# Four projections instead of two beside the token operands, and another buffer ring for the early norms' scratch

## The chip, the cores and the metric

The kernel runs on one core of one Trainium2 chip. The metric is the device time of one execution in microseconds (us), a median over runs. The core's engines each work through a queue of their own, strictly in the order in which the program was written out: TensorE (PE in the profile) multiplies matrices into PSUM, VectorE (DVE), ScalarE (ACT) and GpSimd (POOL) do the elementwise work, and SyncE (SP) mostly issues transfers. TensorE's clock has two levels here, 1.2 and 2.4 GHz; the column PEclk gives the granted clock as a share of the full one.

## The reference, cut to what matters

One step of one decoder layer: RMS norms, one combined input projection, three parallel branches (sparse attention, a pooling mixer, attention to memory), a merge and a gated feed-forward. The change touches only the beginning, the input projection and the norms of single heads:

```python
def project_inputs(x, l, w):
    z = rmsnorm(x, w['attn_norm_g'][l]) @ w['w_in'][l]
    q, kc, vc, ks, vs, kw, vw, nsa_g, pool_u, mem_q, merge_g = jnp.split(z, _split_points(), axis=-1)
    ...
    q = rmsnorm(q.reshape(b, t, KV_HEADS, GROUP, HEAD_DIM), w['nsa_q_g'][l])
    ks = rmsnorm(kv(ks), w['nsa_ks_g'][l])
    kw = rmsnorm(kv(kw), w['nsa_kw_g'][l])
```

1024 prompt tokens and 8 sample tokens go through the same weights, so the kernel handles T = 1032 tokens of width 1024.

## The kernel before, in words

Every factor of a matrix product is held as a sum of a high and a low part (hi + lo), so each product of a 128x128 weight tile with a chunk of tokens takes three matmuls (hi·hi, hi·lo, lo·hi). Tokens lie along the free dimension, in three chunks of 344; the width of 1024 lies in eight tiles k of 128 partitions.

**Stage 1, the token operands (L331 to L359).** For each chunk and each k: a transfer brings `xr`; ScalarE makes `xh` (L338, x times the norm's gain, high part); VectorE makes `xl` (L339, the rest); the squares of `xr` come from ScalarE or GpSimd (L345, L347) and are summed into `ssq` one after the other, by VectorE and GpSimd in turn (L348). Beside it TensorE runs two projections on each chunk as its operands appear (L354, the keys `ks` and `kw`; weights W01). After a chunk, a matmul with ones (L356) gives the sum of squares over partitions in `ps_p`, and the helper `rsqrt` (L273 to L278) makes `rstd`: VectorE scales (L273), ScalarE takes logarithm, exponential and square (L274 to L276), VectorE corrects by one Newton step (L277, L278). L359 then multiplies the projections by `rstd` into `z`.

**After stage 1.** `proj` loads and splits a weight (L239 ScalarE, L240 VectorE) and runs the four query projections q0 to q3 (L257, 72 matmuls each, into the PSUM ring `ps_t`, L364 multiplies by `rstd`). Each of the six tensors ks, kw, q0 to q3 is then normed head by head by `hnorm`, chunk by chunk, so 18 norms: ScalarE squares (L371), splits the square (L239 into `mg`, low part by GpSimd at L240), TensorE sums over a head's partitions by two matmuls (L380, into `ps_s`), `rsqrt` follows (L273 to L278, result `hn_r`), and VectorE applies it (L383). Then come nine V tiles (L257 with `wvh`, `wvl`: 24 matmuls of 280 columns each, into the same ring `ps_t` of three banks); VectorE empties each into `vtok` (L437) and `gate` (L438), and only then does its bank come free for the third tile after it. L474 sums squares of the memory tokens.

**What sets the order.** The Python code is not the order of the engines: the tile framework simulates the program with its own estimates while it builds, and writes each engine's queue out in the order in which that simulation issued the instructions. So a change in one place can reorder queues elsewhere. Buffers are rings: `T` (12 tiles of T columns: `xr`, `ssq`, `z`, V weights), `H` (4 tiles of 512: `rq_w`, `rq_a`, `hn_r`, `vtok`), `U` (10 tiles of 512: squares), `X` (6 of 512), `mg` (5); PSUM has banks in the tags g (1), s (3), t (3) and p (1).

Of the kernel before, what the change touches and what calls it, by code (L numbers as in the profile page):

```python
# [16 lines left out]
KD = D // 128  # L17
# [3 lines left out]
CH = ((0, 344), (344, 344), (688, 344))  # L21
CW = max(n for _, n in CH)
# [8 lines left out]
NT, NH, NU, NX = 12, 4, 10, 6  # L31
# [162 lines left out]
def body(nc, tc, xT, memT, w_p, w_m, w_v, w_mk, w_mv, w_up, w_un, w_out, w_gu, w_dn, w_pool, w_cmp, gains, consts, jlt,  # L194
         pg_k, pg_v, win_k, win_v, cm_k, cm_v, st_p, pt, ptv, o_y, o_k, o_v, o_wk, o_wv, o_pu, o_ps, o_mk, o_mv):
    from contextlib import ExitStack, nullcontext
    V, S, G, PE, SY = nc.vector, nc.scalar, nc.gpsimd, nc.tensor, nc.sync
    f = lambda a: a.bitcast(F32)
# [13 lines left out]
    def XG(name):  # L212
        return xgp.tile([128, T], F32R, name=name, tag="xg", bufs=16)
# [18 lines left out]
    def gv(n, i=0):  # L232
        return gn[:, _GW[n][0] + i:_GW[n][0] + i + 1]

    def psum(tag="s", dt=F32, w=512):
        return pp.tile([128, w], dt, name="ps_" + tag, tag=tag, bufs=dict(zip(('g', 's', 't', 'p'), PSB))[tag])

    def split(src, hi, lo, he=None, le=None):
        (he or S.copy)(hi, src)  # L239
        (le or V.tensor_sub)(lo, src, f(hi))  # L240

    def wload(src, n, eng=None, le=None, parts=1):
        wr = wp.tile([128, n], F32, name="wr", tag="wr", padded_shape=[128, T])
# [38 lines left out]
    ca = A.enter_context(tc.tile_pool(name="cstA", bufs=1))  # L282
    CWID = consts.shape[1]
    ct = ca.tile([128, CWID], F32, name="ct")
    G.dma_start(ct, consts)

    def C(n):
        o, w, r = _CW[n]
# [3 lines left out]
    st_ = {}  # L292
# [3 lines left out]
    def TT(dt=F32, name="t"):  # L296
        return st_["tp"].tile([128, T], dt, name=name, tag="T", bufs=NT)
# [9 lines left out]
    def TU(name):  # L307
        return st_["tp"].tile([128, 512], F32, name=name, tag="U", bufs=NU)

    def TX(name):  # L310
        return st_["tp"].tile([128, 512], F32R, name=name, tag="X", bufs=NX)
# [2 lines left out]
                                               engine=mybir.EngineType.Activation, ins=[], outs=[]))  # L314


    xh, xl, xr = [], [], []
    ssq = TT(name="ssq")
    rstd = cp.tile([128, T], F32, name="rstd")
    W01 = []  # L320
    ks, kw = TT(name="z"), TT(name="z")

    def xload(k, c):
        (SY, S)[k % 2].dma_start(xr[k][:, c], xT[k][:, c])

    for k in range(KD):
        xr.append(TT(name="xr"))
        xh.append(XG("xh"))
        xl.append(XG("xl"))
    for ci, (c0, n) in enumerate(CH):  # L330
        c = slice(c0, c0 + n)  # L331
        pss = [psum("st"[ci % 2])[:, :n] for _ in range(2)]
        for k in range(KD):
            xload(k, c)
            if ci == 0 and k < 2:
                W01.append(wload(w_p[k], 1024, parts=2))
            h, l = xh[k][:, c], xl[k][:, c]
            S.activation(h, xr[k][:, c], AF.Copy, scale=gv("attn", k))  # L338
            V.scalar_tensor_tensor(l, xr[k][:, c], gv("attn", k), f(h), op0=ALU.mult, op1=ALU.subtract)  # L339
            if k == 0:  # L340
                S.activation(ssq[:, c], xr[k][:, c], AF.Square)
            else:
                sq = TU("sq")[:, :n]
                if k in XG_SQ:
                    G.tensor_mul(sq, xr[k][:, c], xr[k][:, c])  # L345
                else:
                    S.activation(sq, xr[k][:, c], AF.Square)  # L347
                (G if k in XG_ADD else V).tensor_add(ssq[:, c], ssq[:, c], sq)  # L348
        for k in range(KD):
            for t in range(2):  # L350
                wh, wl = W01[t]
                w = slice(k * 128, k * 128 + 128)
                for x, (a, b) in enumerate(((wh, xh), (wh, xl), (wl, xh))):
                    PE.matmul(pss[t], lhsT=a[:, w], rhs=b[k][:, c], start=k == 0 and x == 0, stop=k == KD - 1 and x == 2)  # L354
        ps = psum("p")[:, :n]
        PE.matmul(ps, lhsT=ones, rhs=ssq[:, c], start=True, stop=True)  # L356
        rsqrt(tmp, rstd[:, c], ps, n, 1.0 / D)
        for t, z in enumerate((ks, kw)):
            V.tensor_mul(z[:, c], pss[t], rstd[:, c])  # L359

    def proj(i, src=None, tag="t"):
        wh, wl = wload((w_p if src is None else src)[i], 1024)
        z = TT(name="z")
        gemm(wh, wl, xh, xl, KD, lambda ci, c0, n, ps: V.tensor_mul(z[:, c0:c0 + n], ps, rstd[:, c0:c0 + n]),  # L364
             tag)
        return z

    def hnorm(z, blk, inv, g, cols=CH, split_sq=False):
        for c0, n in cols:
            sq = TU("sq")[:, :n]  # L370
            S.activation(sq, z[:, c0:c0 + n], AF.Square)  # L371
            ps = psum("s")[:, :n]
            if not split_sq:
                PE.matmul(ps, lhsT=blk, rhs=sq, start=True, stop=True)
            else:
                hl = mg(n, F32R), mg(n, F32R)
                split(sq, *hl, le=G.tensor_sub)
                bl = blkr if blk is blk64 else onesr
                for x in range(2):
                    PE.matmul(ps, lhsT=bl, rhs=hl[x], start=x == 0, stop=x == 1)  # L380
            r = tmp([128, 512], name="hn_r")[:, :n]
            rsqrt(tmp, r, ps, n, inv)
            V.scalar_tensor_tensor(z[:, c0:c0 + n], z[:, c0:c0 + n], g, r, op0=ALU.mult, op1=ALU.mult)  # L383

    blk64 = C("blk64")
# [5 lines left out]
    ps = psum("g")  # L391
# [1109 lines left out]
```

## Time and profile before

| | |
|---|---|
| median of 3 runs | 1869.57 us (1867.78 to 1874.47) |
| profiled execution, its own time | 1869.54 us |
| its span (first to last instruction) | 1867.8 us |
| TensorE busy | 1798.3 us, 96% of the span |
| VectorE, ScalarE, GpSimd busy | 65%, 47%, 39% |
| TensorE busy in the first 50 us | 33.5 us |
| last matmul of stage 1 (L354) | 48.27 us |
| first matmul of V tile 4 | 116.08 us |

The profile is of one execution; its time lies 1.7 us over its span and within 0.1 us of the median. Times in the trace count from the first instruction. TensorE is the engine that is nearly always busy; the first 50 us are the one stretch of the early program in which it is idle for a third of the time.

### The profile page before, as it was taken

How to read it: one execution, taken by the hardware profiler on the slowest of the kernel's cores; microseconds unless marked ns; L12 is line 12 of the kernel's file. 1: busy time of each engine (PE TensorE's matmuls, PEld its weight loads, DVE VectorE, ACT ScalarE, POOL GpSimd, SP SyncE). 2: the span in 40 equal slices, each digit the busy share in tenths (PEclk: the TensorE clock that was granted, in tenths of full speed). 3: DMA queues.
4: the chain of work that ended last, by engine and by line, in shares of the span. 5: the costliest groups of instructions: out<-in, count | busy, mean ns of one | idle time of the engine just before them, and what ended most of it. 6: DMA issues, size and time to landing. Idle time of an engine off the chain costs nothing.

```text
span 1867.8 us, 34509 instructions
## 1 busy us (share of the span) xinstructions
PE 1798.3 (96%) x12337; PEld 1729.2 (93%) x12337; DVE 1210.0 (65%) x2748; ACT 870.7 (47%) x2012; POOL 737.5 (39%) x865
## 2 busy tenths in 40 slices
PE   6999999999999999989999999999999999999999
PEld 5998998888988999979989998899999999999999
DVE  8875788663564766778886834866666666636332
ACT  5643766445454676657774545422322223314100
POOL 5300211556341645457753437655545545100000
PEclk9999999899999999989999999999999999999999
DMA  4243124999665111552325643122222222546122
GB/s 162 100 148 139 65 101 164 296 316 315 205 201 169 53 43 63 179 165 78 108 64 177 213 134 100 62 87 78 71 80 80 84 87 69 170 131 184 59 69 94
DMA packets 142366, 241.13 MB, mean 129 GB/s; under 512 B 21449, under 2 KB 100450, under 8 KB 142194
## 3 DMA queue, kind: packets, MB, share of 16 engines
q1 hardware_dynamic: 118722, 189.69, 31.2%
q0 software_dynamic: 8496, 30.23, 4.8%
q10 hardware_dynamic: 14976, 19.01, 2.9%
q8 instruction: 97, 1.59, 0.4%
q14 instruction: 75, 0.61, 0.1%
HBM read 176.31 MB, written 62.55 MB: 128 GB/s over the span
## 4 chain that ended last, share of the span: by engine, by line
PE 55%; DMA 5%; DVE 4%; issue 2%; ACT 2%; POOL 1%; SPq 0%; ACTq 0%; DVEq 0%; POOLq 0%
PE ps_t L257 10%; PE ps_s L1385 10%; PE ps_t L1385 9%; PE ps_g L257 7%; PE ps_s L257 7%; PE ps_p L1061 3%; PE ps_s L1032 3%; PE ps_t L1077 2%; PE ps_g L1385 2%; PE ps_p L1385 2%; DMA mg<-acd 1%; DMA mg<-gd 1%; DMA gt<-gd 1%; DMA olr<-od 1%; DVE t L240 0%
## 5 line engine op out<-in xcount | busy, mean ns | idle before, releaser
L257 PE MATMUL ps_g<-xh,wh 128*128 128x344 f32 x624 | 206.1, 330 | 3.9 <-ACT mg L543 2.3
L257 PE MATMUL ps_g<-xl,wh 128*128 128x344 f32 x624 | 201.7, 323 | 0.0
L257 PE MATMUL ps_g<-xh,wl 128*128 128x344 f32 x624 | 201.6, 323 | 0.0
L239 ACT CAST wh<-wr 128x512 fp32r<-128x512 f32 (+3 forms) x138 | 99.9, 746 | 199.9 <-PE ps_t L257 83.5
L1051 POOL TENSOR_SCALAR P<-P,st,gate 128x384 f32<-128x384 f32 (+2 forms) x192 | 125.6, 664 | 94.6 <-DVE st L1046 37.8
L240 DVE TENSOR_TENSOR wl<-wr,wh 128x512 fp32r<-128x512 f32 (+3 forms) x112 | 105.0, 946 | 56.9 <-ACT wh L239 55.5
L239 ACT CAST cw<-tS 128x512 fp32r<-128x512 f32 x88 | 54.3, 619 | 182.0 <-PE ps_t L1385 98.2
L522 ACT ACTIVATE P<-P,st 128x384 f32<-128x384 f32 (+2 forms) x192 | 112.1, 586 | 40.1 <-DVE st L519 36.3
L257 PEld LDWEIGHTS ps_g<-xh,wh 128*128 128x128 f32 x624 | 118.2, 189 | 9.2 <-ACT mg L543 4.1
L257 PEld LDWEIGHTS ps_g<-xl,wh 128*128 128x128 f32 x624 | 118.5, 190 | 1.1 <-issue 0.4
L257 PEld LDWEIGHTS ps_g<-xh,wl 128*128 128x128 f32 x624 | 118.2, 189 | 1.3 <-issue 0.2
L240 DVE TENSOR_TENSOR ptl<-ps_t,pth 128x512 fp32r<-128x512 f32 (+1 forms) x208 | 108.0, 530 | 15.6 <-ACT pth L239 13.4
L239 ACT CAST pth<-ps_t 128x512 fp32r<-128x512 f32 (+1 forms) x208 | 91.3, 457 | 46.6 <-PE ps_t L1077 29.2
L240 DVE TENSOR_TENSOR cw<-tS,cw 128x512 fp32r<-128x512 f32 x88 | 93.3, 1061 | 29.7 <-ACT cw L239 26.1
L1385 PE MATMUL ps_s<-t,cw 128*128 128x258 f32 x792 | 106.1, 283 | 3.1 <-ACT rq L274 3.1
L1385 PE MATMUL ps_t<-t,cw 128*128 128x258 f32 x792 | 106.8, 283 | 2.1 <-DVE t L240 2.1
L1385 PE MATMUL ps_s<-b,cw 128*128 128x258 f32 x792 | 107.8, 286 | 0.0
L1385 PE MATMUL ps_t<-b,cw 128*128 128x258 f32 x792 | 105.6, 282 | 0.3 <-issue 0.3
L1385 PEld LDWEIGHTS ps_s<-t,cw 128*128 128x128 f32 x792 | 100.0, 190 | 3.3 <-ACT rq L274 3.3
L1385 PEld LDWEIGHTS ps_t<-t,cw 128*128 128x128 f32 x792 | 99.6, 189 | 2.9 <-DVE t L240 2.9
L1385 PEld LDWEIGHTS ps_s<-b,cw 128*128 128x128 f32 x792 | 101.4, 192 | 0.3
L519 DVE CUSTOM_DVE_ANT_0 P<-ps_s,ct 128x384 f32<-128x384 f32 (+3 forms) x160 | 83.2, 530 | 27.0 <-PE ps_t L1077 18.1
(527 smaller groups left out, 5659.0 us busy)
## 6 DMA issues: line engine op xcount, KB each, us to landing
kpg<-pg_k SPq DMA_DIRECT2D x128, 192.0 KB, 4.1
wr<-w_gu SPq DMA_DIRECT2D x44, 512.0 KB, 3.8
gd<-mg ACTq DMA_DIRECT2D x72, 172.0 KB, 3.4
wr<-w_m POOLq DMA_DIRECT2D x24, 512.0 KB, 5.4
acd<-zu SPq DMA_DIRECT2D x44, 258.0 KB, 2.0
mg<-acd SPq DMA_DIRECT2D x66, 172.0 KB, 3.0
mg<-gd SPq DMA_DIRECT2D x48, 172.0 KB, 2.4
wr<-w_p SPq DMA_DIRECT2D x16, 512.0 KB, 3.4
```

The costliest lines, as they stand in the source:

```text
L239: (he or S.copy)(hi, src)
L240: (le or V.tensor_sub)(lo, src, f(hi))
L257: PE.matmul(ps, lhsT=x, rhs=y, start=i == 0, stop=i == n - 1)
L519: V.tensor_tensor_reduce(P[u], s, m, -scale, ini, ALU.add, ALU.min, st[:, u:u + 1])
L522: S.activation(P[u], P[u], AF.Exp, bias=nm, scale=-1.0, accum_out=st[:, 6 + u:7 + u])
L1032: PE.matmul(ps, lhsT=u["q"][:, i * 128:i * 128 + 128], rhs=kk[:, k0 * 128 + a:k0 * 128 + a + n], start=x == 0, stop=x == 1)
L1051: lastp[:] = [G.tensor_scalar(p_, p_, st4[:, j, 5:6], gate[:, q, c:c + 1], op0=ALU.mult, op1=ALU.mult)]
L1061: PE.matmul(pv[:, c0:c0 + n], lhsT=lh, rhs=rhs, start=pvs["n"] == 0, stop=last, skip_group_check=True)
L1077: PE.transpose(pt_[:, x * 128:x * 128 + 128], pd[y][:, o - offs[y]:o - offs[y] + 128], ident)
L1385: PE.matmul(ps[c], lhsT=a[:, x * 512 + k * 128:x * 512 + k * 128 + 128], rhs=b[k][:, y * HT + c * HC:y * HT + c * HC + HC], start=first an ...
```

## The change

Four projections (ks, kw, q0, q1) instead of two run on each chunk inside stage 1. For that, the weights of q0 and q1 are loaded whole (`wraw`) and split in halves, into the rings X and U (`w2`, `w3`); the third projection uses the PSUM bank g and the fourth one more of the chunk's tag (s or t). `proj` is left with q2 and q3. The token tiles `xr` take three T tiles a chunk instead of eight for all. The matmul with ones stands behind the third projection. The scratch `rq_w` and `rq_a` of the 18 norms moves from ring H (4 tiles) to ring U (10); `hn_r` stays in H. The line numbers move: L339 becomes L349, L348 L358, L354 L369, L356 L380, L359 L383, L364 L389, L380 L408, L383 L411, L437 L465, L438 L466, L474 L502. The core of the diff:

```diff
@@ constants @@
-    G.dma_start(ct, consts)
...
@@ stage 1 @@
-    xh, xl, xr = [], [], []
-    ssq = TT(name="ssq")
+    xh, xl = [], []
     rstd = cp.tile([128, T], F32, name="rstd")
-    W01 = []
-    ks, kw = TT(name="z"), TT(name="z")
...
+    W = []
+    raws = [TT(name="wraw") for _ in range(2)]
...
+    def halves(raw, new):
+        hl = [[], []]
+        for i in range(2):
+            h, l = new(), new()
+            split(raw[:, i * 512:i * 512 + 512], h, l)
+            hl[0].append(h)
+            hl[1].append(l)
+        return [lambda k, t=t: t[k // 4][:, k % 4 * 128:k % 4 * 128 + 128] for t in hl]
+
     for ci, (c0, n) in enumerate(CH):
         c = slice(c0, c0 + n)
-        pss = [psum("st"[ci % 2])[:, :n] for _ in range(2)]
+        xt = [TT(name="xr") for _ in range(3)]
+        if ci == 0:
+            ssq = TT(name="ssq")
+            zs = [TT(name="z") for _ in range(4)]
+        pss = [psum("sts"[ci])[:, :n] for _ in range(2)]
         for k in range(KD):
-            xload(k, c)
+            xr = xt[k // 3][:, k % 3 * CW:k % 3 * CW + n]
+            (SY, S)[k % 2].dma_start(xr, xT[k][:, c])
...
+        if ci == 0:
+            for t in range(2):
+                SY.dma_start(raws[t][:, :1024], w_p[2 + t])
+            W.append(halves(raws[0], lambda: TX("w2")))
+            W.append(halves(raws[1], lambda: st_["tp"].tile([128, 512], F32R, name="w3", tag="U", bufs=NU)))
+            G.dma_start(ct, consts)
+
+        def along(t, k):
+            wh, wl = W[t]
+            for x, (a, b) in enumerate(((wh, xh), (wh, xl), (wl, xh))):
+                PE.matmul(pss[t], lhsT=a(k), rhs=b[k][:, c], start=k == 0 and x == 0, stop=k == KD - 1 and x == 2)
+
         for k in range(KD):
             for t in range(2):
-                wh, wl = W01[t]
-                w = slice(k * 128, k * 128 + 128)
-                for x, (a, b) in enumerate(((wh, xh), (wh, xl), (wl, xh))):
-                    PE.matmul(pss[t], lhsT=a[:, w], rhs=b[k][:, c], start=k == 0 and x == 0, stop=k == KD - 1 and x == 2)
-        ps = psum("p")[:, :n]
-        PE.matmul(ps, lhsT=ones, rhs=ssq[:, c], start=True, stop=True)
+                along(t, k)
+        pss += [psum("g")[:, :n], psum("sts"[ci])[:, :n]]
+        for t in (2, 3):
+            for k in range(KD):
+                along(t, k)
+            if t == 2:
+                ps = psum("p")[:, :n]
+                PE.matmul(ps, lhsT=ones, rhs=ssq[:, c], start=True, stop=True)
         rsqrt(tmp, rstd[:, c], ps, n, 1.0 / D)
-        for t, z in enumerate((ks, kw)):
+        for t, z in enumerate(zs):
             V.tensor_mul(z[:, c], pss[t], rstd[:, c])
+    ks, kw, q0, q1 = zs
...
@@ norms @@
+    def tmpU(shape, name):
+        return TU(name)[:, :shape[1]]
+
-    def hnorm(z, blk, inv, g, cols=CH, split_sq=False):
+    def hnorm(z, blk, inv, g, cols=CH, split_sq=False, tm=None):
...
-            rsqrt(tmp, r, ps, n, inv)
+            rsqrt(tm or tmp, r, ps, n, inv)
...
-    hnorm(ks, blk64, 1 / 64, gv("ks"), split_sq=True)
+    hnorm(ks, blk64, 1 / 64, gv("ks"), split_sq=True, tm=tmpU)
...
-        q = proj(2 + j)
-        hnorm(q, blk64, 1 / 64, gv("q"), split_sq=True)
+        q = (q0, q1)[j] if j < 2 else proj(2 + j)
+        hnorm(q, blk64, 1 / 64, gv("q"), split_sq=True, tm=tmpU)
```

How the change moves instructions, at the three places that the prediction speaks of.

VectorE's queue in the middle of stage 1. Before, this is what stands around the `rsqrt` of chunk 0 (`rq_w_296`); `xl` are low parts of chunks 1 and 2:

```order
L339 SCALAR_TENSOR_TENSOR xl_172<-xr_170,gn_139,xh_171 128x344
L339 SCALAR_TENSOR_TENSOR xl_169<-xr_167,gn_139,xh_168 128x344
L273 TENSOR_SCALAR rq_w_296<-ps_p_294 128x344
L339 SCALAR_TENSOR_TENSOR xl_178<-xr_176,gn_139,xh_177 128x344
L707 TENSOR_SCALAR pts_3812<-pts_3812 1x128
L711 TENSOR_SCALAR ptr_3815<-ptr_3815 128x16
L339 SCALAR_TENSOR_TENSOR xl_175<-xr_173,gn_139,xh_174 128x344
L348 TENSOR_TENSOR ssq_154<-ssq_154,sq_339 128x344
```

After, around the `rsqrt` of chunk 0 (`rq_w_363`, `rstd_153`), whose four products z are at L383; `xr_375` holds chunk 1:

```order
L273 TENSOR_SCALAR rq_w_363<-ps_p_337 128x344
L277 TENSOR_TENSOR rq_w_363<-rq_w_363,rq_a_364 128x344
L278 SCALAR_TENSOR_TENSOR rstd_153<-rq_w_363,rstd_153 128x344
L383 TENSOR_TENSOR z_176<-ps_s_180,rstd_153 128x344
L383 TENSOR_TENSOR z_177<-ps_s_181,rstd_153 128x344
L383 TENSOR_TENSOR z_178<-ps_g_311,rstd_153 128x344
L383 TENSOR_TENSOR z_179<-ps_s_312,rstd_153 128x344
L349 SCALAR_TENSOR_TENSOR xl_157<-xr_375,gn_139,xh_156 128x344
L358 TENSOR_TENSOR ssq_175<-ssq_175,sq_387 128x344
```

The low parts of later chunks stood ahead of and inside the first `rsqrt` before; now the first `xl` of chunk 1 comes behind the whole `rsqrt` and the four products of chunk 0. The `rsqrt` of chunk 1 stands in the new queue behind all of chunk 2's low parts and sums.

VectorE's queue in the middle of the 18 norms. L273 begins the VectorE part of a norm, L277 and L278 end its `rsqrt`, L383 (after: L411) applies it. Before:

```order
L273 TENSOR_SCALAR rq_w_648<-ps_s_640 128x344
L277 TENSOR_TENSOR rq_w_629<-rq_w_629,rq_a_630 128x344
L278 SCALAR_TENSOR_TENSOR hn_r_628<-rq_w_629,hn_r_628 128x344
L383 SCALAR_TENSOR_TENSOR z_157<-z_157,gn_139,hn_r_628 128x344
L273 TENSOR_SCALAR rq_w_757<-ps_s_749 128x344
L277 TENSOR_TENSOR rq_w_648<-rq_w_648,rq_a_649 128x344
L278 SCALAR_TENSOR_TENSOR hn_r_647<-rq_w_648,hn_r_647 128x344
L364 TENSOR_TENSOR z_813<-ps_t_866,rstd_155 128x344
L383 SCALAR_TENSOR_TENSOR z_157<-z_157,gn_139,hn_r_647 128x344
```

After:

```order
L273 TENSOR_SCALAR rq_w_930<-ps_s_922 128x344
L277 TENSOR_TENSOR rq_w_930<-rq_w_930,rq_a_931 128x344
L278 SCALAR_TENSOR_TENSOR hn_r_929<-rq_w_930,hn_r_929 128x344
L411 SCALAR_TENSOR_TENSOR z_179<-z_179,gn_139,hn_r_929 128x344
L273 TENSOR_SCALAR rq_w_949<-ps_s_941 128x344
L277 TENSOR_TENSOR rq_w_949<-rq_w_949,rq_a_950 128x344
L278 SCALAR_TENSOR_TENSOR hn_r_948<-rq_w_949,hn_r_948 128x344
L411 SCALAR_TENSOR_TENSOR z_179<-z_179,gn_139,hn_r_948 128x344
```

Before, the L273 of a norm stands ahead of the L277 of the norm before it; now each norm's L273, L277, L278 and L411 stand together, and the next norm's L273 behind them. This holds from the fourth norm to the last; the first `vtok` and `gate` stand behind the L273 of norm 18, as before.

TensorE's queue around the end of V tile 3 (`wvh`, `wvl`; the third of the V tiles that fill the ring `ps_t`). Before:

```order
L257 MATMUL ps_t<-wvl,xh 128x280
L257 MATMUL ps_t<-wvh,xl 128x280
L257 MATMUL ps_t<-wvh,xh 128x280
L257 MATMUL ps_t<-wvl,xh 128x280
L257 MATMUL ps_t<-wvh,xl 128x280
L474 MATMUL ps_s<-sq,ones 128x256 x8
L257 MATMUL ps_t<-wvh,xh 128x280
L257 MATMUL ps_t<-wvl,xh 128x280
```

After:

```order
L257 MATMUL ps_t<-wvh,xh 128x280
L257 MATMUL ps_t<-wvl,xh 128x280
L257 MATMUL ps_t<-wvh,xl 128x280
L408 MATMUL ps_s<-mg,blkr 128x344 x25
L502 MATMUL ps_s<-sq,ones 128x256 x8
L408 MATMUL ps_s<-mg,blkr 128x344
L257 MATMUL ps_t<-wvh,xh 128x280
L257 MATMUL ps_t<-wvl,xh 128x280
```

Before, the norms' matmuls (L380) were spread over the query projections and the first V tiles, the last of them inside V tile 3. Now five norms have theirs among q2, q3 and the V tiles, and the other 13 stand in one block behind V tile 3, with no projection between them, ahead of V tile 4. The memory's sums (L502, before L474) stand at the block's end. V tile 4 is the 561st TensorE instruction in both queues.

## Rows read from the trace of the kernel before

**Rows 1.** The page's head and first part: span, busy time of each engine.

```profile
span 1867.8 us, 34509 instructions
PE 1798.3 (96%) x12337; PEld 1729.2 (93%) x12337; DVE 1210.0 (65%) x2748; ACT 870.7 (47%) x2012; POOL 737.5 (39%) x865
```

**Rows 2.** Busy us and instructions by stretch; then PEclk, DMA share, GB/s.

```profile
0.00:50.00 50.00, 33.54 (x162) 29.80 (x163) 39.31 (x66) 26.77 (x53) 25.95 (x28) 0.97 0.46 157
40.00:50.00 10.00, 8.04 (x40) 7.74 (x41) 7.95 (x13) 4.70 (x9) 3.94 (x4) 0.83 0.14 53
48.40:116.00 67.60, 66.35 (x430) 65.31 (x428) 57.19 (x107) 49.55 (x101) 18.32 (x17) 1.00 0.34 127
300.00:400.00 100.00, 91.77 (x515) 84.32 (x513) 70.14 (x180) 50.42 (x149) 45.62 (x100) 0.93 0.83 275
```

**Rows 3.** What TensorE waited for, 0 to 120 us: total us, times, longest.

```profile
PE ps_s L354 <- ACT xh L338: 7.7, 1, 7.7
...
PE ps_t L354 <- DVE xl L339: 1.9, 3, 0.8
...
PE ps_t L257 <- DVE gate L438: 1.3, 1, 1.3
```

**Rows 4.** TensorE in time (start, us) around V tile 4; idle before in brackets.

```profile
110.93 0.29 PE L257 MATMUL ps_t<-wvh,xl 128*128 128x280 f32 x1
111.06 3.69 PE L474 MATMUL ps_s<-sq,ones 128*128 128x256 f32 x16
116.08 0.37 PE L257 MATMUL ps_t<-wvh,xh 128*128 128x280 f32 x1 [1.33 <-DVE gate L438]
```

**Rows 5.** TensorE in time, the end of stage 1.

```profile
43.94 0.49 PE L354 MATMUL ps_s<-xl,wh 128*128 128x344 f32 x1
44.23 0.49 PE L354 MATMUL ps_s<-xh,wl 128*128 128x344 f32 x1
...
48.27 0.33 PE L354 MATMUL ps_s<-xh,wl 128*128 128x344 f32 x1
48.44 0.32 PE L257 MATMUL ps_t<-xh,wh 128*128 128x344 f32 x1
```

**Rows 6.** VectorE's groups, 0 to 120 us: busy us, mean ns, idle before.

```profile
L339 DVE SCALAR_TENSOR_TENSOR xl<-xr,gn,xh 128x344 fp32r<-128x344 f32 x24 | 20.3, 880 | 0.7 <-ACT xh L338 0.4 <-DMA xr<-xT 0.3
...
L348 DVE TENSOR_TENSOR ssq<-ssq,sq 128x344 f32<-128x344 f32 x12 | 9.3, 777 | 0.8 <-POOL ssq L348 0.8
...
L240 DVE TENSOR_TENSOR wl<-wr,wh 128x512 fp32r<-128x512 f32 x4 | 3.2, 830 | 2.1 <-ACT wh L239 2.1
```

**Rows 7.** VectorE in time, the first low part.

```profile
8.65 0.57 DVE L339 SCALAR_TENSOR_TENSOR xl<-xr,gn,xh 128x344 fp32r<-128x344 f32 x1
```

**Rows 8.** VectorE in time, two products by rstd.

```profile
54.98 0.94 DVE L359 TENSOR_TENSOR z<-ps_s,rstd 128x344 f32<-128x344 f32 x2
```

**Rows 9.** VectorE in time, one norm from L273 to L383, and a gate.

```profile
107.62 0.50 DVE L273 TENSOR_SCALAR rq_w<-ps_s 128x344 f32<-128x344 f32 x1
...
110.11 0.52 DVE L277 TENSOR_TENSOR rq_w<-rq_w,rq_a 128x344 f32<-128x344 f32 x1
110.66 0.52 DVE L278 SCALAR_TENSOR_TENSOR hn_r<-rq_w,hn_r 128x344 f32<-128x344 f32 x1
111.22 0.58 DVE L383 SCALAR_TENSOR_TENSOR z<-z,gn,hn_r 128x344 f32<-128x344 f32 x1
...
115.70 0.23 DVE L438 TENSOR_SCALAR gate<-ps_t,rtok 128x24 f32<-128x24 f32 x1
```

**Rows 10.** ScalarE in time, first and last of five steps without a break.

```profile
76.85 0.54 ACT L274 ACTIVATE rq_a<-ps_s,epst 128x344 f32<-128x344 f32 x1
...
78.42 0.49 ACT L276 ACTIVATE rq_a<-hn_r 128x344 f32<-128x344 f32 x1
```

**Rows 11.** VectorE in time, an L277.

```profile
75.01 1.07 DVE L277 TENSOR_TENSOR rq_w<-rq_w,rq_a 128x344 f32<-128x344 f32 x1
```

**Rows 12.** GpSimd in time, beside it.

```profile
74.77 0.93 POOL L240 TENSOR_TENSOR mg<-sq,mg 128x344 fp32r<-128x344 f32 x1 [2.13 <-PE ps_s L380]
```

More of the change, by code (lines that the diff above doesn't have):

```diff
@@ L314, in body @@
                                                engine=mybir.EngineType.Activation, ins=[], outs=[]))
-    xh, xl, xr = [], [], []
-    ssq = TT(name="ssq")
+    xh, xl = [], []
     rstd = cp.tile([128, T], F32, name="rstd")
-    W01 = []
-    ks, kw = TT(name="z"), TT(name="z")
-    def xload(k, c):
-        (SY, S)[k % 2].dma_start(xr[k][:, c], xT[k][:, c])
+    W = []
+    raws = [TT(name="wraw") for _ in range(2)]
     for k in range(KD):
-        xr.append(TT(name="xr"))
         xh.append(XG("xh"))
         xl.append(XG("xl"))
+    def halves(raw, new):
[6 more added lines that the diff above has]
+        return [lambda k, t=t: t[k // 4][:, k % 4 * 128:k % 4 * 128 + 128] for t in hl]
     for ci, (c0, n) in enumerate(CH):
         c = slice(c0, c0 + n)
-        pss = [psum("st"[ci % 2])[:, :n] for _ in range(2)]
+        xt = [TT(name="xr") for _ in range(3)]
[3 more added lines that the diff above has]
+        pss = [psum("sts"[ci])[:, :n] for _ in range(2)]
         for k in range(KD):
-            xload(k, c)
+            xr = xt[k // 3][:, k % 3 * CW:k % 3 * CW + n]
+            (SY, S)[k % 2].dma_start(xr, xT[k][:, c])
             if ci == 0 and k < 2:
-                W01.append(wload(w_p[k], 1024, parts=2))
+                wh, wl = wload(w_p[k], 1024, parts=2)
+                W.append([lambda k, t=t: t[:, k * 128:k * 128 + 128] for t in (wh, wl)])
             h, l = xh[k][:, c], xl[k][:, c]
-            S.activation(h, xr[k][:, c], AF.Copy, scale=gv("attn", k))
-            V.scalar_tensor_tensor(l, xr[k][:, c], gv("attn", k), f(h), op0=ALU.mult, op1=ALU.subtract)
+            S.activation(h, xr, AF.Copy, scale=gv("attn", k))
+            V.scalar_tensor_tensor(l, xr, gv("attn", k), f(h), op0=ALU.mult, op1=ALU.subtract)
             if k == 0:
-                S.activation(ssq[:, c], xr[k][:, c], AF.Square)
+                S.activation(ssq[:, c], xr, AF.Square)
             else:
@@ L344, in body @@
                 if k in XG_SQ:
-                    G.tensor_mul(sq, xr[k][:, c], xr[k][:, c])
+                    G.tensor_mul(sq, xr, xr)
                 else:
-                    S.activation(sq, xr[k][:, c], AF.Square)
+                    S.activation(sq, xr, AF.Square)
                 (G if k in XG_ADD else V).tensor_add(ssq[:, c], ssq[:, c], sq)
+        if ci == 0:
[8 more added lines that the diff above has]
+                PE.matmul(pss[t], lhsT=a(k), rhs=b[k][:, c], start=k == 0 and x == 0, stop=k == KD - 1 and x == 2)
         for k in range(KD):
             for t in range(2):
-                wh, wl = W01[t]
-                w = slice(k * 128, k * 128 + 128)
-                for x, (a, b) in enumerate(((wh, xh), (wh, xl), (wl, xh))):
-                    PE.matmul(pss[t], lhsT=a[:, w], rhs=b[k][:, c], start=k == 0 and x == 0, stop=k == KD - 1 and x == 2)
-        ps = psum("p")[:, :n]
-        PE.matmul(ps, lhsT=ones, rhs=ssq[:, c], start=True, stop=True)
+                along(t, k)
[6 more added lines that the diff above has]
+                PE.matmul(ps, lhsT=ones, rhs=ssq[:, c], start=True, stop=True)
         rsqrt(tmp, rstd[:, c], ps, n, 1.0 / D)
-        for t, z in enumerate((ks, kw)):
+        for t, z in enumerate(zs):
             V.tensor_mul(z[:, c], pss[t], rstd[:, c])
+    ks, kw, q0, q1 = zs
     def proj(i, src=None, tag="t"):
@@ L402, in body @@
     V.tensor_copy(ksn[:, 0], ks[:, TP:T])
-    hnorm(kw, blk64, 1 / 64, gv("kw"), split_sq=True)
+    hnorm(kw, blk64, 1 / 64, gv("kw"), split_sq=True, tm=tmpU)
     SY.dma_start(o_k[3], kw)
```

## The prediction

> **What bounds the kernel now.** I read the page first. TensorE is busy for 96% of the span [rows 1], so what ends late for TensorE ends late for the kernel. The table of stretches then shows the one early place where it is not: in the first 50 us it is busy for 33.5 us, so 16.5 us are idle [rows 2]. The waits say why: 7.7 us for the first xh, which is the start itself, and short ones for the low parts xl [rows 3]; ScalarE, VectorE and GpSimd are making operands. Behind that TensorE is full: 66.4 us of the 67.6 us from 48.4 to 116 [rows 2]. In those same 67.6 us all 18 head norms run on VectorE and ScalarE, covered by the matmuls of q0 to q3 and of three V tiles: 67.6 / 18 = 3.76 us a norm. The one wait that shows through is V tile 4, which waits 1.33 us, until 116.08, for a `gate` that empties the first V tile's bank [rows 4]. That `gate` stands on VectorE behind the L273 of norm 18. So the cover was about as long as the norms; any norm that is late now moves V tile 4. Behind it TensorE has little slack for a long time.
>
> **What the change moves.** TensorE's own work is the same. 144 matmuls (q0, q1) go from behind stage 1 into it; at 0.16 us from start to start (0.17 from 48.27 to 48.44 in [rows 5]; 66.35 us for 430 of mixed width, 0.154, in [rows 2]) these are 23.0 us of cover that the norms lose. Two things follow, when the norms can start and how fast they run.
>
> *The end of stage 1, called P.* The fences show that the new queue of VectorE finishes chunk 0, its `rsqrt` and four products, before the first low part of chunk 1. Its steps:
> - Chunk 0 from 8.65 us [rows 7]: 8 low parts at 0.88 = 7.0, 4 sums at 0.78 = 3.1, two weight halves still to split and four new ones at 0.83 = 5.0, and 2.1 of idle as before for weights [rows 6]; to which I add 1 for the two weights more that have to be fetched. That gives 26.9.
> - `rsqrt`, from L273 to the instruction behind L278: 3.6 (107.62 to 111.22, [rows 9]); four products at 0.47 [rows 8] = 1.9: 32.4.
> - Chunks 1 and 2: 16 low parts = 14.1 and 8 of the serial sums = 6.2, with 0.8 of idle for GpSimd's part of the sums [rows 6]: 53.5.
> - The `rsqrt` of chunk 1, 3.6, stands behind all of that, then three products, 1.4: 58.5. Only the third empties bank g, for which chunk 2's third projection waits. 49 matmuls remain, 24 + 1 + 24: 7.8 at 0.16. About 1 more for a low clock: at 43.94 a matmul took 0.29 from start to start [rows 5], in a stretch with a granted clock of 0.83 [rows 2].
> - P = 67. Before, the last matmul of stage 1 began at 48.27 [rows 5]; with the 144 matmuls it would be 71.4. Stage 1 as such therefore gains 4 us.
>
> The bounds: a low part without contention takes 0.57 [rows 7] instead of 0.88, which over 16 is 5 us less (62); if each took 1.07, the length of a contended VectorE instruction [rows 11], 3 more, and two further us if the weights are late (72).
>
> *The cover behind P.* q2 and q3 (144 x 0.16 = 23.0), ten norm matmuls (1.6) and three V tiles (72 at 0.13, from [rows 4], = 9.4) are 34.0, plus 3 us for their waits at the start and between (the first norms' squares and the weight of q2 follow P too): V tile 3 ends at P + 37. In TensorE's queue five norms have their matmuls by then. Norm 6 has its L273 at P + 37.6. Thirteen norms are left, with nothing beside them.
>
> *The pace of these.* In the new queue each norm's L273, L277, L278 and L411 stand together. So ScalarE's part lies between the first two, not beside another norm. One cycle: four VectorE steps at 0.55 from start to start (110.11, 110.66, 111.22, [rows 9]) = 2.2, and ScalarE's five instructions without a break, the next norm's square and cast among its own three, from 76.85 to 78.42 + 0.49 = 2.06 [rows 10]. That is 4.26. A single norm of before agrees: 107.62 to 111.22 + 0.58 = 4.18 [rows 9]. To this comes a collision. GpSimd makes the low part of the next norm's square just as ScalarE ends, and L277 has two inputs from SBUF: beside GpSimd's 74.77 to 75.70 [rows 12] it took 1.07 [rows 11] instead of 0.52 [rows 9]. I take it for nearly every norm, +0.5: 4.75. From norm 6 to norm 18 are 12 cycles: 57.0. The bounds are 3.76, the pace of before (45.1), and 5.3, where L278 is hit too (63.6).
>
> *The sum.* L273 of norm 18 at 67 + 37.6 + 57.0 = 161.6; its end, `vtok` and `gate` about 1 us: V tile 4 begins at 162.6 instead of 116.1, 46.5 later. TensorE has then done little for 50 us; from [rows 5] a low clock costs 0.13 a matmul, so 1 to 2 us: +48. The profiled execution, 1869.5, is within 0.1 us of the median, so the forecast is 1917.5, rounded 1917.
>
> *Edits at no cost.* The scratch in ring U instead of H removes a limit of four tiles, but the queue as written no longer asks for two norms at once, so it cannot help; no instruction is added, so it cannot hurt. The constants' transfer keeps its place in GpSimd's queue. The token tiles by chunk bring the same bytes; DMA is little used behind 20 us, and chunk 2's tiles must wait for chunk 0's to be used (by 27), five to ten us ahead of need. If that cover were gone, P would move by what is late, within its 72. The two weights are loaded earlier, not additionally.
>
> **The Trainium skill speaks for the change.** In the first 50 us VectorE is the busiest engine (39.3 us), in the 67.6 behind it TensorE (66.4, [rows 2]). The Trainium skill, Perfetto Trace Analysis, Optimization Strategy, says that a kernel whose most-contended engine changes over time may gain by interleaving those regimes; this change interleaves them, and by that rule alone the time would fall.
>
> **Rivals.**
> - *It gains (the other side).* The 144 matmuls fill stage 1's idle time. By P alone, 4 us: 1865; if all 16.5 us idle [rows 2] were filled, 1853. That is what the rule just named would give. For it: the idle time is real. Against it: it needs V tile 4 no later than 116, so 12 cycles in 116 - 67 - 37.6 - 1 = 10.4 us, 0.87 a norm, where VectorE's four instructions alone take 2.2. It decides when a norm costs less than that; the fences exclude it unless V tile 4 doesn't wait for norm 18. Chance 0.04.
> - *No change that counts,* 1860 to 1879 (0.5%, 9 us, is about what a measurement of this kernel tells from nothing): it needs norms of some 1.7 us. Chance 0.03.
> - *Part is given back.* Later stretches have idle TensorE time that doesn't follow from TensorE, such as 8.2 us from 300 to 400 with DMA at 0.83 [rows 2]. Transfers that need only free buffers run ahead during the 48 us, and then waits are shorter. Or the norms keep the pace of before: 12 less. 1897 to 1908. Chance 0.2.
> - *It is worse.* P at 72, cycles of 5.3: 5 + 6.6 more, 1929, up to 1935. Chance 0.13.
>
> **How the numbers follow.** The forecast, within 9 us of 1917, has a chance of 0.6. Faster by over 0.5%: 0.04; within: 0.03; slower: 0.93. The range from 1899 to 1929 takes in the forecast, most of the part given back and half of the worse case.
>
> **What would show it.** TensorE's table: stage 1 ends near 67, full until about 104, then nearly idle until about 160, waiting for `mg` (L408, from GpSimd and ScalarE) and last for a `gate` L466. VectorE: L273, L277, L278, L411 repeating every 4.7 us, L277 waiting for ScalarE's L276. The granted clock falls in that stretch. I am wrong if V tile 4 starts before 145, if the norms overlap on VectorE, or if the time lost up to there isn't there at the end.

## The result, and the profile after

The changed kernel took 1915.01 us (median of 5 runs, 1909.62 to 1917.25) against 1871.72 us for the kernel before (5 runs): a ratio of 1.0223, 95% interval 1.0206 to 1.0240 (a ratio here is taken over all runs; it is not the quotient of the two medians). It is slower, by 43.3 us between the medians, where 48 were forecast. Its profiled execution took 1910.71 us, 41.2 more than that of before.

The head of the page, first part, and the clock row of the 40 slices:

```profile
span 1909.0 us, 34529 instructions
PE 1808.0 (95%) x12337; PEld 1730.5 (91%) x12337; DVE 1221.1 (64%) x2750; ACT 871.7 (46%) x2014; POOL 734.3 (38%) x865
...
PEclk9958999999999999999999999999999999999999
```

TensorE's busy time grew by 9.7 us ([rows 1]: 1798.3), the span by 41.2 us. The third slice, 95 to 143 us, has a granted clock of 0.5, the lower of the two levels: TensorE was idle for most of it. The table of stretches (columns as in [rows 2]) shows where:

```profile
0.00:50.00 50.00, 40.65 (x228) 38.63 (x229) 37.60 (x66) 26.16 (x53) 23.13 (x28) 1.00 0.48 168
61.00:96.60 35.60, 35.60 (x246) 35.56 (x245) 20.69 (x36) 14.82 (x30) 5.05 (x5) 1.00 0.30 107
96.60:159.60 63.00, 20.93 (x45) 11.36 (x43) 33.95 (x62) 27.48 (x64) 11.51 (x13) 0.57 0.13 51
```

Stage 1 became what the change promises: 40.7 us busy in the first 50 against 33.5 [rows 2]. From 61 to 96.6 TensorE is full. Then come 63 us with 21 us of work, at a granted clock of 0.57. What TensorE waited for up to 170 us (total, times, longest):

```profile
PE ps_s L408 <- ACT mg L239: 35.6, 12, 3.1
...
PE ps_s L408 <- POOL mg L240: 5.2, 11, 1.1
PE ps_t L257 <- DVE gate L466: 1.2, 1, 1.2
```

40.8 us of waits for `mg`, the norms' squares, where before no norm was waited for [rows 3]. TensorE in time around that stretch, from the end of V tile 3 to V tile 4:

```profile
96.47 0.29 PE L257 MATMUL ps_t<-wvh,xl 128*128 128x280 f32 x1
96.60 0.67 PE L408 MATMUL ps_s<-mg,blkr 128*128 128x344 f32 x2
...
147.25 0.65 PE L408 MATMUL ps_s<-mg,blkr 128*128 128x344 f32 x1 [3.07 <-ACT mg L239]
148.31 0.65 PE L408 MATMUL ps_s<-mg,blkr 128*128 128x344 f32 x1 [0.41 <-POOL mg L240]
152.04 0.65 PE L408 MATMUL ps_s<-mg,blkr 128*128 128x344 f32 x1 [3.07 <-ACT mg L239]
152.49 5.71 PE L502 MATMUL ps_s<-sq,ones 128*128 128x256 f32 x16
157.85 0.51 PE L408 MATMUL ps_s<-mg,blkr 128*128 128x344 f32 x1
159.60 0.37 PE L257 MATMUL ps_t<-wvh,xh 128*128 128x280 f32 x1 [1.24 <-DVE gate L466]
```

One pair of L408 every 4.8 us (147.25 to 152.04), and V tile 4 at 159.60 instead of 116.08 [rows 4]. The groups of VectorE and, below, the first of ScalarE from 96.6 to 158 us (busy, mean ns, idle before) show two engines that wait for each other:

```profile
L277 DVE TENSOR_TENSOR rq_w<-rq_w,rq_a 128x344 f32<-128x344 f32 x13 | 12.5, 959 | 26.5 <-ACT rq_a L276 26.5
L411 DVE SCALAR_TENSOR_TENSOR z<-z,gn,hn_r 128x344 f32<-128x344 f32 x13 | 7.5, 575 | 0.4
L278 DVE SCALAR_TENSOR_TENSOR hn_r<-rq_w,hn_r 128x344 f32<-128x344 f32 x13 | 7.3, 564 | 0.4
L273 DVE TENSOR_SCALAR rq_w<-ps_s 128x344 f32<-128x344 f32 x12 | 6.1, 509 | 0.0
```

```profile
L274 ACT ACTIVATE rq_a<-ps_s,epst 128x344 f32<-128x344 f32 x12 | 6.6, 549 | 28.6 <-DVE rq_w L273 28.6
```

L277 waits 26.5 us for ScalarE, and ScalarE's L274 waits 28.6 us for VectorE. One cycle on VectorE, and GpSimd beside its L277:

```profile
140.15 0.51 DVE L273 TENSOR_SCALAR rq_w<-ps_s 128x344 f32<-128x344 f32 x1
142.85 0.99 DVE L277 TENSOR_TENSOR rq_w<-rq_w,rq_a 128x344 f32<-128x344 f32 x1 [2.19 <-ACT rq_a L276]
143.88 0.52 DVE L278 SCALAR_TENSOR_TENSOR hn_r<-rq_w,hn_r 128x344 f32<-128x344 f32 x1
144.43 0.58 DVE L411 SCALAR_TENSOR_TENSOR z<-z,gn,hn_r 128x344 f32<-128x344 f32 x1
144.92 0.51 DVE L273 TENSOR_SCALAR rq_w<-ps_s 128x344 f32<-128x344 f32 x1
```

```profile
142.56 0.91 POOL L240 TENSOR_TENSOR mg<-sq,mg 128x344 fp32r<-128x344 f32 x1 [3.86 <-ACT mg L239]
```

From L273 to L273 are 4.77 us: 2.70 to L277, 1.03 through it, then 0.55 and 0.49. L277 lasts 0.99 with GpSimd at work from 142.56 to 143.47. Of the 18 norms, 16 have an L277 of 0.96 to 1.25 us; that of norm 18, with no GpSimd instruction beside it, takes 0.52.

### The profile page after: what moved, and what is told of

The parts are those of the page before. It is cut to its first block, busy times and chain, and to the rows that moved or that the text cites. A ratio compares the mean times of both kernels' runs of the same rounds, so it can differ in the third digit from the quotient of the medians.

```text
span 1909.0 us, 34529 instructions
## 1 busy us (share of the span) xinstructions
PE 1808.0 (95%) x12337; PEld 1730.5 (91%) x12337; DVE 1221.1 (64%) x2750; ACT 871.7 (46%) x2014; POOL 734.3 (38%) x865
## 4 chain that ended last, share of the span: by engine, by line
PE 60%; DMA 9%; DVE 5%; issue 2%; ACT 2%; POOL 1%; SPq 1%; ACTq 0%; POOLq 0%; DVEq 0%
PE ps_g L257 10%; PE ps_t L257 9%; PE ps_s L1413 9%; PE ps_t L1413 9%; PE ps_s L257 6%; PE ps_p L257 3%; PE ps_p L1089 3%; PE ps_s L1060 3%; PE ps_t L1105 2%; DMA kpg<-pg_k 2%; DMA mg<-acd 2%; PE ps_g L1413 2%; PE ps_p L1413 2%; DMA vpg<-pg_v,ptr 1%; DMA mg<-gd 1%
## 5 line engine op out<-in xcount | busy, mean ns | idle before, releaser
L257 PE MATMUL ps_g<-xh,wh 128*128 128x344 f32 x624 | 204.9, 328 | 3.5 <-ACT mg L571 1.5
L257 PE MATMUL ps_g<-xh,wl 128*128 128x344 f32 x624 | 200.8, 322 | 0.0
L257 PE MATMUL ps_g<-xl,wh 128*128 128x344 f32 x624 | 200.5, 321 | 0.0
L1079 POOL TENSOR_SCALAR P<-P,st,gate 128x384 f32<-128x384 f32 (+2 forms) x192 | 125.6, 663 | 94.9 <-DVE st L1074 40.8
L550 ACT ACTIVATE P<-P,st 128x384 f32<-128x384 f32 (+2 forms) x192 | 112.5, 588 | 40.1 <-DVE st L547 35.6
L257 PEld LDWEIGHTS ps_g<-xh,wh 128*128 128x128 f32 x624 | 117.5, 188 | 8.1 <-ACT mg L571 3.5
L257 PEld LDWEIGHTS ps_g<-xl,wh 128*128 128x128 f32 x624 | 117.7, 189 | 1.2 <-issue 0.2
L257 PEld LDWEIGHTS ps_g<-xh,wl 128*128 128x128 f32 x624 | 117.5, 188 | 1.4
L240 DVE TENSOR_TENSOR cw<-tS,cw 128x512 fp32r<-128x512 f32 x88 | 92.8, 1057 | 33.5 <-ACT cw L239 29.7
L240 POOL TENSOR_TENSOR mg<-sq,mg 128x344 fp32r<-128x344 f32 x30 | 31.0, 1033 | 199.6 <-ACT mg L239 190.2
```

Of the source, the lines that this page charges most:

```text
L257: PE.matmul(ps, lhsT=x, rhs=y, start=i == 0, stop=i == n - 1)
L550: S.activation(P[u], P[u], AF.Exp, bias=nm, scale=-1.0, accum_out=st[:, 6 + u:7 + u])
L1079: lastp[:] = [G.tensor_scalar(p_, p_, st4[:, j, 5:6], gate[:, q, c:c + 1], op0=ALU.mult, op1=ALU.mult)]
```

## The experiments

Each run is told with its median and its ratio to the kernel before on the same chip. The table gives three times of the profiled executions: when V tile 4 begins, when the projections of the merge gates begin (the first `ps_g` matmul of L257), and when the selected-block stage begins (first matmul with `khh`), and how much later than before the latter two are. They come from one execution each, and for two kernels it lies far from the median: E2's took 1871.62 us (median 1884.84), E3's 1884.77 us (median 1874.83).

| kernel | projections, scratch | V tile 4 | gate projections | `khh` | ratio (interval) |
|---|---|---|---|---|---|
| before | 2, H | 116.1 | 183.7 | 600.7 | 1 |
| changed | 4, U | 159.6 | 226.9 (+43.2) | 638.2 (+37.5) | 1.0223 (1.0206 to 1.0240) |
| E1 | 2, U | 156.2 | 223.5 (+39.8) | 639.1 (+38.4) | 1.0208 (1.0190 to 1.0226) |
| E2 | 4, H | 121.1 | 188.6 (+4.9) | 604.8 (+4.1) | 1.0063 (1.0046 to 1.0079) |
| E3 | 4, X | 113.8 | 183.9 (+0.2) | 606.6 (+5.9) | 1.0012 (0.9994 to 1.0029) |
| E7 | 2, X | 115.0 | 184.0 (+0.3) | 603.1 (+2.4) | 1.0004 (0.9993 to 1.0016) |
| E4 | 4, X, V tiles early | 74.2 | 178.8 (-4.9) | 601.5 (+0.8) | 1.0016 (1.0001 to 1.0031) |
| E8 | 4, H, V tiles early | 74.3 | 186.9 (+3.2) | 603.5 (+2.8) | 1.0048 (1.0031 to 1.0065) |
| E6 | 4, U, V tiles early | 74.2 | 231.5 (+47.8) | 646.8 (+46.1) | 1.0279 (1.0262 to 1.0296) |
| E5 | 4, U, low part on VectorE | 146.9 | 215.2 (+31.5) | 635.7 (+35.0) | 1.0244 (1.0216 to 1.0271) |
| E9 | 4, U, squares in X | 112.6 | 179.9 (-3.8) | 597.0 (-3.7) | 1.0011 (0.9994 to 1.0028) |
| E10 | 4, only rq_a in U | 162.7 | 230.3 (+46.6) | 644.2 (+43.5) | 1.0258 (1.0221 to 1.0294) |

**E1, the ring alone.** The kernel before, with `tmpU` for the norms of ks, kw and q:

```diff
-            rsqrt(tmp, r, ps, n, inv)
+            rsqrt(tm or tmp, r, ps, n, inv)
...
-        hnorm(q, blk64, 1 / 64, gv("q"), split_sq=True)
+        hnorm(q, blk64, 1 / 64, gv("q"), split_sq=True, tm=tmpU)
```

> The kernel before with one edit alone: the norms' scratch rq_w, rq_a from ring U, still two projections beside stage 1. VectorE's queue is then written with the norms one behind another, and TensorE's queue has nine norms in a block behind V tile 3. Theory (the ring sets the serial order, and the serial order is most of the loss): V tile 3 ends at about 111 as before, eight cycles of 4.8 us and 5 us for the memory's sums and the evictions follow, V tile 4 starts at about 155 instead of 116; time 1905 to 1912. Rival (the loss comes from the moved projections alone, the ring does not matter): V tile 4 near 116, time 1866 to 1876.

1912.44 us. TensorE in time, from the end of V tile 3:

```profile
108.48 0.29 PE L257 MATMUL ps_t<-wvh,xl 128*128 128x280 f32 x1
...
143.76 0.65 PE L383 MATMUL ps_s<-mg,blkr 128*128 128x344 f32 x1 [3.07 <-ACT mg L239]
...
148.54 0.65 PE L383 MATMUL ps_s<-mg,blkr 128*128 128x344 f32 x1 [3.07 <-ACT mg L239]
149.00 5.80 PE L477 MATMUL ps_s<-sq,ones 128*128 128x256 f32 x16
...
156.20 0.37 PE L257 MATMUL ps_t<-wvh,xh 128*128 128x280 f32 x1 [1.24 <-DVE gate L441]
```

The same picture as in the changed kernel, one norm every 4.78 us (143.76 to 148.54), with not one projection moved. V tile 4 came at 156.2 (about 155 was expected), the time 0.4 us above the expected range. The ring's edit alone makes nearly all of the loss: 1.0208 against 1.0223, with intervals that overlap.

**E2, the projections alone.** The changed kernel without `tm=tmpU`.

> The changed kernel with the norms' scratch back in ring H, four projections beside stage 1. The norms are then written overlapped, six of them behind V tile 3. Theory: stage 1 ends at 61 as in the changed kernel, the last six norms go at 2 to 3 us each, V tile 4 starts at 112 to 116; time 1862 to 1872. Rival (the cover that the norms lost is the loss, at any ring): six cycles of 4.8 behind 97 put V tile 4 at 131, time about 1885; if the ring changes nothing at all, 1915.

1884.84 us. The theory's time (1862 to 1872) was missed, and the median is the rival's 1885; but V tile 4 came at 121.1, between theory (112 to 116) and rival (131), and no norm took the rival's 4.8 us. TensorE in time:

```profile
110.23 0.94 PE L408 MATMUL ps_s<-mg,blkr 128*128 128x344 f32 x2 [1.78 <-ACT rq_a L274]
112.69 0.94 PE L408 MATMUL ps_s<-mg,blkr 128*128 128x344 f32 x2 [1.51 <-ACT rq_a L274]
114.86 6.25 PE L502 MATMUL ps_s<-sq,ones 128*128 128x256 f32 x16 [1.23 <-ACT rq_a L274]
121.06 0.37 PE L257 MATMUL ps_t<-wvh,xh 128*128 128x280 f32 x1
```

The last six norms have their matmuls 2.4 to 3.6 us apart, overlapped, near the theory's 2 to 3; but the sums of the memory tokens, behind them in the queue, took 6.25 us (granted clock 0.58 from 114.8 to 121 us) instead of the 3.69 of [rows 4], which the expectation had not counted. At the gate projections 4.9 us are lost. This trace is of the fastest of the five executions, 1871.62 us; the other four took 1883.0 to 1887.9. Where they lost another 11 us and more was not seen, so the agreement with the rival's time has no shown cause.

**E3, E4 and E7, a third ring.** `tmpU` takes its tiles from ring X (six tiles, used by `w2` in stage 1 and free after it):

```diff
     def tmpU(shape, name):
-        return TU(name)[:, :shape[1]]
+        return st_["tp"].tile([128, 512], F32, name=name, tag="X", bufs=NX)[:, :shape[1]]
```

E3 is the changed kernel with this; E7 the kernel before with it; E4 is E3 with the block of the nine V tiles moved in the code ahead of `hnorm(ks, ...)`.

> The changed kernel with the norms' scratch in ring X (six tiles, free once stage 1 is done) instead of U, so neither with hn_r in H nor with the squares in U. Theory (in U the scratch takes the buffers that let squares run ahead; it is not that H was left): overlapped norms, three behind V tile 3, V tile 4 at 105 to 112; time 1858 to 1868. Rival (any larger ring than H makes the order serial): V tile 4 near 160, time about 1915.

> As the one with ring X, and the nine V tiles written ahead of the norms, so that no gate stands behind a norm on VectorE. Theory: stage 1 ends at 61, where the same matmuls would have been done at 71.4 before; nothing waits for the norms until q2, q3 and the next projections are through, so the 10.5 us of stage 1 stay; time 1856 to 1864. Rival (what stage 1 gains is lost again behind the norms wherever they stand): 1868 to 1875.

> The kernel before with the norms' scratch in ring X, two projections beside stage 1: the base for the changed kernel with ring X. Theory (what the four projections gain in stage 1, 10 us, the norms that start 10 us later take again): gate projections begin at 182 to 185, as in the kernel before and as with four projections in ring X; time 1868 to 1876, the same. Rival (four projections as such gain or lose): a difference of over 5 us at the gate projections between two and four projections.

E3: 1874.83 us, V tile 4 at 113.8. The order is overlapped, so it is not that the scratch left H; but no gain came (1858 to 1868 was expected, with V tile 4 at 105 to 112). E7: 1875.09 us, as expected; at the gate projections two and four projections differ by 0.1 us, so what the four gain in stage 1 the later norms take again. E4: 1876.65 us, not the 1856 to 1864 expected: it was 4.9 us ahead at the gate projections, and this was gone before `khh`. One row shows the place: the transfers of the cache pages (`kpg`, the form of the issuing instruction, first and last start), in the kernel before, then in E4:

```profile
L724 SPq DMA_DIRECT2D kpg<-pg_k x128: 327/333/1132, 316.2 to 431.3; - x128
```

```profile
L752 SPq DMA_DIRECT2D kpg<-pg_k x128: 328/333/1493, 311.4 to 431.5; - x128
```

E4 issues its first page 4.8 us earlier and its last at the same time, in a stretch where DMA is busy at 0.83 [rows 2]. The early start brought nothing there; that the transfers set that stage's pace is argued from this, not shown by a run of its own. E9 (below) did otherwise:

```profile
L752 SPq DMA_DIRECT2D kpg<-pg_k x128: 332/333/1113, 312.5 to 427.3; - x128
```

Its first page was issued 3.7 us earlier than in the kernel before and its last 4.0 earlier, and it still was 3.7 ahead at `khh`. It lost that later: its last `khh` matmul began at 980.0, against 979.8 in the kernel before.

**E6 and E8, the V tiles early with U and with H.** The same move of the V tiles as in E4.

> The changed kernel, scratch in ring U, with the nine V tiles written ahead of the norms. V tile 4 then waits for no norm. Theory (the length of the serial chain is the loss, V tile 4 only the place where it shows): V tiles done at 93, the norms still one behind another at 4.77, seven of them beside q2, q3 and a projection, eleven in a block behind; the wait moves there, gate projections begin at 225 to 235 against 183.7 before, time 1910 to 1922. Rival (the gate behind norm 18 is the loss): as with ring X and early V tiles, 1870 to 1880.

> Four projections, ring H, V tiles ahead of the norms: norms overlapped, in pairs beside q2, q3 and the next projections. Theory: nothing waits for a norm; gate projections begin at 178 to 181, some 4 us ahead of before, of which the stage of the page loads, whose DMA is busy at 0.8 to 0.9, leaves 0 to 3; time 1868 to 1876. Rival (an early gain reaches the end): 1862 to 1867.

E6: 1925.23 us, 3 over the expected range. No V tile waits for a norm, and the time is still lost, behind q2, q3 and the first projection after them, where TensorE waits 33.5 us for `mg` (columns as in [rows 2]):

```profile
145.00:195.00 50.00, 17.10 (x38) 9.97 (x38) 25.79 (x49) 20.98 (x52) 8.54 (x9) 0.56 0.09 36
```

V tile 4 was the place, the serial chain the cause. E8: 1881.49 us; the expectation was missed (1868 to 1876), with the gate projections 3.2 us late instead of early. The longest wait between 90 and 190 us is a new one, a projection's bank whose product stands on VectorE behind the last norms and, from 152.4 to 158.1 us, the operands of the memory tokens:

```profile
PE ps_t L257 <- DVE z L389: 9.5, 1, 9.5
```

**E9 and E10, what the ring has to do with it.** E9 leaves the scratch in U and takes the norms' squares out of it; E10 leaves the squares in U and only half of the scratch:

```diff
# E9
-            sq = TU("sq")[:, :n]
+            sq = (st_["tp"].tile([128, 512], F32, name="sq", tag="X", bufs=NX) if tm else TU("sq"))[:, :n]
# E10
-        return TU(name)[:, :shape[1]]
+        return TU(name)[:, :shape[1]] if name == "rq_a" else tmp(shape, name=name)
```

> The changed kernel with the norms' scratch in ring U as it is, and the norms' squares moved out of U into ring X instead. Theory (scratch and squares in one ring is what makes the order serial, not ring U as such): the norms are written overlapped, the last of them inside V tile 3, V tile 4 at 98 to 105, time 1868 to 1878. Rival (the scratch in ring U is serial by itself): cycles of 4.77, V tile 4 near 160, time 1910 to 1917.

> The changed kernel with only rq_a in ring U and rq_w back in ring H: 18 scratch tiles share the ring with the squares instead of 36. Theory (one shared tile a norm is enough: a square can no longer run ahead of the norm before it): still serial, 13 norms behind V tile 3, V tile 4 at 155 to 162, time 1908 to 1918. Rival (it is the number of tiles in the ring, ten for three a norm): half the scratch gives overlap back, time 1870 to 1890.

E9: 1876.22 us, overlapped, the last norm matmul at 104.5 inside V tile 3; V tile 4 at 112.6 instead of 98 to 105, because the memory's sums stand between. E10: 1920.63 us, 2.6 over the expected range, and serial. So it is the sharing: scratch in U without the squares (E9) and squares in U without the scratch (E2, E3) are overlapped, both together are serial, with three tiles a norm or with two. ScalarE in time shows it, first the squares in the changed kernel:

```profile
66.19 0.48 ACT L399 ACTIVATE sq<-z 128x344 f32<-128x344 f32 x1
...
73.08 0.49 ACT L399 ACTIVATE sq<-z 128x344 f32<-128x344 f32 x1
...
79.81 0.48 ACT L399 ACTIVATE sq<-z 128x344 f32<-128x344 f32 x1
```

then in E2, and in E9:

```profile
61.21 2.40 ACT L399 ACTIVATE sq<-z 128x344 f32<-128x344 f32 x6 [1.75 <-DVE z L383]
...
63.88 1.63 ACT L399 ACTIVATE sq<-z 128x344 f32<-128x344 f32 x4
```

```profile
61.53 2.40 ACT L399 ACTIVATE sq<-z 128x344 f32<-128x344 f32 x6 [1.75 <-DVE z L383]
```

Apart from the scratch, the squares run ahead: six to ten of them in one go when stage 1 is over. In the same ring with it they come one at a time, each with the norm before it. As I read it, no norm's sum is then ready early, and the simulation writes VectorE's queue norm by norm; what it decides inside was not looked at.

**E5, the collision with GpSimd.** The low part of a norm's square is made on VectorE:

```diff
-                split(sq, *hl, le=G.tensor_sub)
+                split(sq, *hl, le=V.tensor_sub if tm else G.tensor_sub)
```

> The changed kernel with one edit: the low part of the norms' squares is made by VectorE instead of GpSimd. It stands on VectorE between a norm's L273 and L277, where VectorE waits 2.2 us for ScalarE; the order stays serial. Theory (a cycle is four steps of VectorE, 2.2, and ScalarE's run, 2.06; the rest, 0.5, is L277 beside GpSimd): a cycle of 4.2 to 4.3 instead of 4.77, L277 at 0.52, V tile 4 at about 153, time 6 us under the changed kernel, 1904 to 1911. Rival (the 0.5 is not GpSimd's, or one more instruction lengthens the chain): a cycle of 4.77 to 5.3, time 1911 to 1920.

VectorE in time, one cycle:

```profile
122.55 0.51 DVE L273 TENSOR_SCALAR rq_w<-ps_s 128x344 f32<-128x344 f32 x1
122.98 0.57 DVE L411 SCALAR_TENSOR_TENSOR z<-z,gn,hn_r 128x344 f32<-128x344 f32 x1
...
124.80 0.52 DVE L240 TENSOR_TENSOR mg<-sq,mg 128x344 fp32r<-128x344 f32 x1 [0.88 <-ACT mg L239]
125.23 0.51 DVE L277 TENSOR_TENSOR rq_w<-rq_w,rq_a 128x344 f32<-128x344 f32 x1
125.78 0.52 DVE L278 SCALAR_TENSOR_TENSOR hn_r<-rq_w,hn_r 128x344 f32<-128x344 f32 x1
126.22 0.51 DVE L273 TENSOR_SCALAR rq_w<-ps_s 128x344 f32<-128x344 f32 x1
```

The cycle fell to 3.67 (122.55 to 126.22), more than expected. L277 takes 0.51 instead of 0.99, and the next step starts 0.55 behind it instead of 1.03: the collision, 0.48. All 18 norms have an L277 of 0.50 to 0.52 here. Another 0.6 comes from the queue, which now has L273 ahead of the apply at L411: from L278 to L273 are 0.44 instead of 1.04. V tile 4 began at 146.9, 12.7 us earlier than in the changed kernel. But the time was 1921.08 us, not 1904 to 1911: of the 12.7 us, 2.5 are left at `khh`, and at the end of the span it is 10.6 us behind the changed kernel. That is one execution each; the ratios, 1.0244 and 1.0223, have intervals that overlap, so what is shown is that no gain is left. The traces show where it goes: E5's last `khh` matmul begins 9.1 us later (1029.2 against 1020.1). By operations and tile names, its queues of TensorE and VectorE have another order than all the other kernels up to 1024 us, while the others agree with one another from 617 us on at the latest. That this order costs the time is likely, not shown; which part of it would is open.

## Why the prediction was right, and where it was wrong

**The serial chain: right.** It named the place (V tile 4 behind norm 18), the repeating four steps, and a cycle of 4.75; measured 4.77. Its parts hold too: 2.70 to L277 against 0.55 + 2.06, and 0.5 for GpSimd (E5 takes it away). What made the chain serial it had not asked; see below.

**P, mis-sized.** Forecast 67, measured 60.99, the start of q2's first matmul:

```profile
60.83 0.32 PE L369 MATMUL ps_s<-xh,w 128*128 128x344 f32 x1
60.99 0.32 PE L257 MATMUL ps_t<-xh,wh 128*128 128x344 f32 x1
```

VectorE in time gives the parts:

```profile
22.90 0.52 DVE L273 TENSOR_SCALAR rq_w<-ps_p 128x344 f32<-128x344 f32 x1 [1.59 <-PE ps_p L380]
...
27.89 0.90 DVE L349 SCALAR_TENSOR_TENSOR xl<-xr,gn,xh 128x344 fp32r<-128x344 f32 x1
...
48.04 0.51 DVE L273 TENSOR_SCALAR rq_w<-ps_p 128x344 f32<-128x344 f32 x1
```

The `rsqrt` of chunk 0 began at 22.90, not at 26.9: the first low part came at 6.70 instead of 8.65, and up to 22.4 us a low part took 0.70 on average (forecast 0.88), a weight half 0.68 (0.83). From it to the first low part of chunk 1 took 5.0 (forecast 5.5), chunks 1 and 2 20.2 (21.1), and the last 49 matmuls ran at the full clock (granted 1.00 from 52.6 to 61 us), without the 1 us added. So stage 1 gained 10.4 us, not 4. "DMA is little used behind 20 us" was misread: its share was 0.40 from 20 to 30 us, before and after (0.39); ScalarE made chunk 2's `xh` without a wait all the same.

**The block behind V tile 3.** The cover was 35.6 us (forecast 37). Missing in the sum, though the queue stood in the text, was that the memory's sums (L502) stand between the two matmuls of norm 18. They took 5.71 us at a granted clock of 0.64 (152.4 to 158.4 us), against 3.69 [rows 4]: norm 18 waited about 4 us for them. So 159.6 came out, against 162.6, from errors of -6 (P), -1.4 (cover) and +4 (the sums) and a small rest. That the forecast came so near owes something to luck: these errors cancel in part. Behind V tile 4 nothing was lost to a low clock, for which 1 to 2 us had been added: the granted clock is 1.00 from 159.6 to 166 us. Of the 43.5 us, 2.3 came back by the end, less than the rival "part is given back" had.

**What was wrong: the ring "at no cost".** The prediction took the written order as given, and put its loss on the 23 us of cover that moved. "It cannot help ... it cannot hurt", it said of ring U. E1 shows the contrary: ring U alone, with all cover in place, costs 39.8 us at the gate projections. The moved cover alone costs there 4.9 with ring H (E2, whose time is 10 us longer between the medians), 3.4 on top of ring U (43.2 against 39.8), and nothing with ring X (E3 against E7). Total and mechanism of the chain were right; the edit that caused it was the one priced at zero.

**The rival that it gains.** The Trainium skill, Perfetto Trace Analysis, Optimization Strategy, says that interleaving regimes may help. Here stage 1 itself gained 10.4 us. At the gate projections, with the norms overlapped, 4.9 (E4) and 3.8 (E9) are left of it, nothing in E3, and E2 and E8 are late; no run here carries a gain to the end (E4 1.0016, E9 1.0011).

## What to carry to other kernels

Where a scheduler writes the queues, a change of a buffer's ring is a change of order: look at who shares the new ring, and whether something that ran ahead can still do so. Price the pieces of a change one by one, the harmless ones too; here one kernel with a single edit would have told it. And a few microseconds won early are not yet won: follow them through the later stages. In E4 they were gone at the end of the page transfers, in E9 at the end of the `khh` stage.

## What the runs showed that I had not expected

A wider home for scratch made the kernel slower: ten tiles shared with the squares gave 4.77 us a norm, where four tiles of ring H gave 2.4 to 3.6 (the last six of E2). Doing more on VectorE made a cycle shorter (E5: 3.67): the added subtraction lay in its wait and took GpSimd's collision away, and the queue came out in a better order. And a local gain can leave no sign at the end: against the changed kernel, V tile 4 came 12.7 us earlier in E5, and the time was no shorter (1.0244 against 1.0223). No version here is faster than the kernel before.
